# Attention over 64 heads on one core: one PSUM tile for all score buffers, and the order of every engine read from a table

## The chip, the core and the metric

The kernel runs on one core of a Trainium2 chip. A core has five engines, each with its own in-order queue of instructions: TensorE (PE in the profile; PEld are its weight loads), VectorE (DVE), ScalarE (ACT), GpSimd (POOL) and SyncE (SP, which here only issues DMAs). They wait for each other through semaphores. SBUF is the working memory, and PSUM the small memory into which TensorE writes and from which ScalarE and VectorE read. The metric is the device time of one execution in microseconds, lower is better, as the median of several runs.

## The reference

```python
batch, heads, seq, dim = 8, 8, 512, 64          # q, k, v: (8, 8, 512, 64) float32
scale = 1.0 / np.sqrt(dim)
scores = np.einsum('bhqd,bhkd->bhqk', q, k) * scale
scores = scores - scores.max(axis=-1, keepdims=True)
attn = np.exp(scores)
attn = attn / attn.sum(axis=-1, keepdims=True)
out = np.einsum('bhqk,bhkd->bhqd', attn, v)
```

64 independent heads of 512 x 512 attention. The kernel leaves the maximum out, since a constant shift of the scores cancels in the quotient.

## The kernel before

**Tiling.** The 64 heads are taken as 32 pairs g = 0 to 31, with heads a and b. Per head the 512 keys are cut into four chunks c of 128. A block (g, c, head) is a 128 keys x 512 queries piece of the scores; two blocks make a group m, so that a pair has four groups, and group m belongs to pair m // 4. The last group is split into two halves by queries, 127 and 128. A pair in the middle takes its blocks as a0 b0, a1 b1, and so on: the two heads lie on partitions 0 to 63 and 64 to 127, and their two score matmuls run side by side on the two halves of the array. In pairs 0 and 31 the order is a0 a1, a2 a3, b0 b1, b2 b3.

**Steps of a pair.** SyncE loads q, k and v of the pair (256 KB each, seven pairs of buffers each). GpSimd casts them to fp16 (`cast`, L515 and L525). TensorE transposes q and k (`transposes`, L558, two parts of four), and VectorE copies the result from PSUM (`copy`, L571). For each group TensorE makes the scores (`scores`, L598, two matmuls) in a PSUM buffer `st`. There are three such buffers, each 128 x 1024 fp32 (two banks), taken in turn, so the scores of group m wait until group m-3 has been read. Then one engine reads the buffer:

- ScalarE takes the exponential of 110 groups with one ACTIVATE of 128 x 1024 each (L602), into an fp16 tile `pt`.
- For 16 groups, listed in `ON_DVE`, VectorE does it: `raise` (L625) reads PSUM and makes an integer whose bits are a rough 2^x, and five passes (`pass_`, L642 to L665) over fp16 in SBUF make of it two summands, `pe` and `pd`.

**Values.** A unit is 128 queries of one head: four matmuls with `pt` as weights and v, with a column of ones, as the moving side (`values`, L704); a block that VectorE made has two summands, so it takes two matmuls. Seven units share a PSUM bank (tags x0 and x1, two banks in turn; the transposes use them too). VectorE then takes the reciprocal of the sums (`rec`, L671) and multiplies (`mul`, L676) into a ring of results in SBUF, from which SyncE stores. The last head (31 b) has its own four parts (`last_values`, L720), reciprocal (L733), multiplication (L734) and store (L740).

**What sets the order.** Every engine runs the instructions in the order in which the code writes them down. `Plan` writes it: a small simulation in steps of 5 ns with one clock per engine, with prices and rules as constants (`SLOT`, `EXP`, `LATE_COPY`, `HURRY` and others). It decides at each moment which job each engine takes next, and returns the list of steps. The list is played by these lines:

```python
        plan = Plan(groups, NP, 3)
        steps = plan.run()
        ...
        for what, *args in steps:
            do[what](*args)
```

A cast is held behind a VectorE instruction (`cast_behind`, "behind" counts back from the newest), because both engines use the same port of SBUF.

**Waits.** The tile framework adds the semaphores: whoever reads a tile waits for its writer, and whoever takes a buffer again waits for the readers of what was in it. Since each `st` is a tile of its own, two groups in different buffers have no dependence.

Of the kernel before, what the change touches and what calls it, by code (L numbers as in the profile page):

```python
# [17 lines left out]
class Plan:  # L18

    SLOT, EXP, EXP_DONE, EXP_FIXED = 216, 853, 181, 64  # L20
    INTO, OUT_OF = 96, 96
    TRANSPOSE, V_UNIT = 222, 128
    TO_ACT, TO_DVE, TO_PE = 220, 210, 60

    COPY, NORM, RAISE = (601, 690), (50, 133), (1132, 1215)
    RECIPROCAL = 115
    SCALE, PRODUCT, EXTRA = 333, 600, 29
    COPY_1 = (400, 190)
    NORM_COLUMN, PASS_DONE = 67, 115
    PASSES = (SCALE, SCALE, PRODUCT, SCALE, PRODUCT)  # L30
    BITS = 2
    NEEDS = (None, None, 0, 2, 3)
    FIRST_EXP = 5000
    STEP = 5
    CALM, KEEN = 9000, 4
    FIRST_UNIT = 4
    KNOWN, OVER = (13, 15, 18, 20, 22, 24, 27, 42, 50, 61, 69, 97), 6
    ON_DVE = (5, 10, 16, 25, 28, 39, 44, 54, 63, 66, 74, 81, 91, 96, 103, 116)

    LATE_NORM, LATE_COPY, HURRY, SOON, BACKLOG = 700, 1500, 800, 160, 600  # L40
    LATE_MUL, WAIT = 400, 200
    SLACK, AHEAD = 0, 2

    CAST, CAST_PORT, CAST_DONE, TO_POOL = 557, 475, 130, 150
    SCALE_PORT, PRODUCT_PORT, GAP, REACH = 271, 537, 20, 5
    FIRST_LAND, LOAD, STORE, LATENCY, ISSUE = 5200, 752, 376, 2300, 470
    QUEUED, URGENT = 3500, 16
    PAIRED, STORE_ISSUE = 18, 520
    RAW, QK16, NV, NU = 7, 5, 12, 112
    PAIR, DUEK, DUEV, DUEL, PRE = 3300, 3550, 6000, 5000, 0  # L50

    def __init__(self, groups, pairs, first):
        self.groups, self.pairs = groups, pairs
        self.pe, self.act, self.dve = 7000, self.FIRST_EXP, 6300
        self.pool, self.port, self.dma = 4600, 4600, self.FIRST_LAND
        self.m, self.tiled = first, True
        self.read = []
        self.exps = {}
        for m in range(first):
            self.act += self.EXP + self.EXP_FIXED  # L60
            self.exps[m] = self.act + self.EXP_DONE
            self.read.append(self.exps[m])
        self.tq = {0: 5800}
        self.transposed = {0: 5800}
        self.next_t = 1
        self.part_t = 0
        self.banks = [5100, 5800]
        self.todo = [(g, h) for g in range(pairs) for h in range(2)]
        self.last = self.todo.pop()
        self.last_part = 0  # L70
        self.head = None
        self.units = self.FIRST_UNIT
        self.member = {b: m for m, grp in enumerate(groups) for b in grp}
        self.ready = []
        self.passes = []
        self.passed = {}
        self.raised = set()
        self.steps = []
        self.busy_dve = 0
        self.order, self.paired = [], 0  # L80

        late = {grp[0][0] for m, grp in enumerate(groups) if m in self.ON_DVE}
        due = []
        for g in range(pairs):
            scores = 5000 + self.PAIR * g
            if g:
                due += [(scores - self.DUEK, g, "k"), (scores - self.DUEK + 10, g, "q")]
            due.append((scores + self.DUEV + (self.DUEL if g in late else 0), g, "v"))
        self.due = sorted(due)
        self.uncast = list(self.due)  # L90
        self.casts = []
        self.landed, self.cast_done = {}, {}
        self.first_loads = [(g, n) for _, g, n in self.due if g < self.RAW]
        self.first_loads += [(self.RAW, "k"), (self.RAW, "q")]
        for x in self.first_loads:
            self.dma += self.LOAD
            self.landed[x] = self.dma
        self.loads, self.stores, self.stored = [], [], []
        self.sp = 1650 + 470 * len(self.first_loads)

    def note(self, t, *what):
        self.steps.append((t, len(self.steps)) + what)

    def trigger(self, t):

        ops = self.ops
        if not ops or ops[-1][1] <= t - 300:  # L110
            return 1, None
        n = len(ops) - 1
        while (
            n > 0
            and len(ops) - n < self.REACH
            and not ops[n][2]
            and ops[n][0] - ops[n - 1][1] <= self.GAP
        ):
            n -= 1
        if n > 0 and ops[n][0] - ops[n - 1][1] <= self.GAP:  # L120
            n -= 1
        return len(ops) - n, ops[n][1]

    def emit(self, t, back, after):
        _, g, n = self.uncast.pop(0)
        shared = (g, n) == (1, "q")
        self.note(t, "cast", g, n, back if t > self.CALM else 0)
        if not shared:
            self.casts.append((g, n, t if after is None else after + self.TO_POOL))
        if g + self.RAW < self.pairs:  # L130
            self.loads.append((g + self.RAW, n))

    def fits(self, t, soon=0):
        if not self.uncast:
            return False
        _, g, n = self.uncast[0]
        if n != "v" and g >= self.QK16 and self.transposed.get(g - self.QK16, 1e9) > t:
            return False
        return self.landed.get((g, n), 1e9) <= t + soon

    def step_pool(self, t):
        if self.uncast and self.uncast[0][1:] != (1, "q") and not self.casts and self.pool <= t:
            quiet = not self.passes and self.port <= t and not any(x[1] == "raise" for x in self.ready)
            if self.fits(t) and (quiet or self.uncast[0][0] - self.PRE < t):
                self.emit(t, 1, None)
        if self.casts and self.pool <= t and self.port <= t:
            g, n, after = self.casts[0]
            if after <= t and self.landed.get((g, n), 1e9) <= t:
                self.casts.pop(0)
                begin = max(self.pool, self.port, after, self.landed[(g, n)])  # L150
                self.pool = begin + self.CAST
                self.port = begin + self.CAST_PORT
                self.cast_done[(g, n)] = begin + self.CAST + self.CAST_DONE

    def step_sp(self, t):
        if self.sp > t or (self.loads and self.dma > t + self.QUEUED):
            return
        urgent = len(self.stores) > self.URGENT
        if self.loads and not urgent:
            g, n = self.loads[0]  # L160
            if self.cast_done.get((g - self.RAW, n), 1e9) <= t:
                self.loads.pop(0)
                self.note(t, "load", g, n)
                self.dma = max(self.dma, t + self.LATENCY - self.LOAD) + self.LOAD
                self.landed[(g, n)] = self.dma
                self.sp = t + self.ISSUE
                return
        if self.stores and self.stores[0] <= t:
            both = self.both()
            if both and (len(self.stores) < 2 or self.stores[1] > t):  # L170
                return
            heads = 2 if both else 1
            self.note(t, "store", heads)
            self.dma = max(self.dma, t + self.LATENCY - heads * self.STORE) + heads * self.STORE
            for _ in range(heads):
                self.stores.pop(0)
                self.stored.append(self.dma)
            self.paired += heads - 1
            self.sp = t + self.STORE_ISSUE

    def both(self):

        n = len(self.stored)
        g, h, u = self.order[n]
        return (
            self.paired < self.PAIRED
            and g < self.pairs - 2
            and h == 0
            and n + 1 < len(self.order)
            and self.order[n + 1][0] == g  # L190
            and u % self.NU + 8 <= self.NU
        )

    def room(self, t, u):
        heads = (u - self.NU - self.FIRST_UNIT + 3) // 4
        return heads <= 0 or len(self.stored) >= heads and self.stored[heads - 1] <= t

    def free(self, n=0):
        m = self.m + n
        if m >= len(self.groups):  # L200
            return 1e9
        g = self.groups[m][0][0]
        return max(0 if m < 3 else self.read[m - 3], self.tq.get(g, 1e9))

    def for_dve(self, m):
        return m in self.ON_DVE
# [692 lines left out]
```

## Time and profile before

| what | value |
|---|---|
| time, median of 3 runs | 113.66 us (113.52 to 114.11) |
| time of the profiled execution | 113.92 us |
| its span, from first to last instruction | 112.1 us |
| TensorE, VectorE, ScalarE, GpSimd busy | 103.2, 100.8, 105.5, 65.9 us |
| granted TensorE clock, mean | 0.994 |
| moved by DMA | 33.84 MB |

How to read it: a row of the timeline has the start in us, the length in us, the engine, the line and operation, the tiles (written <- read), the shape and how many instructions were merged in the row. In brackets stands how long the engine had been idle before it, and which instruction ended that. An instruction's length covers its whole stay in the engine, so lengths of neighbours overlap. Busy shares near 100% on three engines say that none can be off for long; they do not say which one sets the end.

### The profile page before, as it was taken

Reading aid. Unit: us, or ns where it says so; the run is one execution under the profiler, and the core shown is the slowest. Engines: PE = TensorE matmul, PEld = TensorE weight load, DVE = VectorE, ACT = ScalarE, POOL = GpSimd, SP = SyncE. Lnnn points to the kernel's source line nnn. Section 1 sums busy time; section 2 is a strip of 40 time slices with the busy share of each in tenths; the row PEclk is TensorE's granted clock in tenths of the full one; section 3 lists DMA queues with packets and bytes.
Section 4 is the critical chain, followed back from the end, with each engine's and each line's share of the span. In section 5 each row is a group of like instructions: output and inputs, shape, how many; then the busy total and the mean of one; then the engine's idle time right before and its main releaser. Section 6 shows DMA issues by size and latency. Waiting matters only on the chain.

```text
span 112.1 us, 4408 instructions
## 1 busy us (share of the span) xinstructions
PE 103.2 (92%) x1728; PEld 69.4 (62%) x1728; DVE 100.8 (90%) x227; ACT 105.5 (94%) x118; POOL 65.9 (59%) x127
## 2 busy tenths in 40 slices
PE   7978889999799998999989999899999999999980
PEld 7634555766367766658647767577557577675660
DVE  1647999999999999999999999999999999997390
ACT  4599999999999999999999999999999999999970
POOL 2147768549756886495594786876784855600000
PEclk9999999999999999999999999999999999999997
DMA  3999999999999999999999999999999974142354
GB/s 106 276 359 353 345 350 347 355 336 349 345 347 336 341 346 343 354 364 375 370 358 382 350 355 377 354 372 362 343 366 305 349 245 143 52 141 99 97 167 161
DMA packets 35093, 33.84 MB, mean 302 GB/s; under 512 B 2304, under 2 KB 35072, under 8 KB 35072
## 3 DMA queue, kind: packets, MB, share of 16 engines
q1 hardware_dynamic: 34496, 33.04, 90.4%
q10 hardware_dynamic: 576, 0.52, 1.4%
q8 instruction: 13, 0.21, 0.8%
q14 instruction: 8, 0.07, 0.2%
HBM read 25.17 MB, written 8.39 MB: 299 GB/s over the span
## 4 chain that ended last, share of the span: by engine, by line
DVE 39%; PE 24%; DMA 15%; issue 8%; POOL 7%; SPq 3%; ACT 2%; POOLq 0%; ACTq 0%
PE o L704 13%; DMA v<-in_v_dram 10%; PE st L598 8%; DVE pd L625 8%; DVE tqk L571 7%; DVE ring L676 7%; DMA q<-in_q_dram 5%; DVE m L659 4%; POOL qkp L525 4%; DVE pd L665 4%; POOL vp L515 3%; PE tp L558 2%; SPq L509 2%; DVE m L642 2%; DVE pe L651 2%
## 5 line engine op out<-in xcount | busy, mean ns | idle before, releaser
L602 ACT ACTIVATE pt<-st 128x1024 f16<-128x1024 f32 (+1 forms) x110 | 100.3, 1144 | 0.2 <-PE st L598 0.2
L704 PEld LDWEIGHTS <-pt 128*128 128x128 f16 x880 | 38.8, 98 | 12.1 <-issue 10.2
L704 PE MATMUL o<-vp,pt 128*128 128x65 f16 x880 | 45.3, 194 | 0.4 <-POOL vp L515 0.2
L598 PE MATMUL st<-tqk 64*128 64x512 f16 (+1 forms) x250 | 41.7, 380 | 2.6 <-ACT pt L602 1.4
L525 POOL CAST qkp<-k 128x512 f16<-128x512 f32 x31 | 22.2, 717 | 11.3 <-DVE rc L671 5.3
L525 POOL CAST qkp<-q 128x512 f16<-128x512 f32 x30 | 21.7, 725 | 9.0 <-DVE rc L671 5.3
L515 POOL CAST vp<-v 128x512 f16<-128x512 f32 x32 | 21.4, 679 | 9.2 <-PE st L598 2.4
L676 DVE TENSOR_TENSOR ring<-o,rc 128x448 f32<-128x448 f32 (+2 forms) x37 | 22.3, 606 | 0.4
L704 PE MATMUL o<-vp,pe 128*128 128x65 f16 x128 | 21.8, 194 | 0.0
L704 PE MATMUL o<-vp,pd 128*128 128x65 f16 x128 | 21.7, 192 | 0.0
L558 PE MATMUL tp<-ident,qkp 128*128 128x128 f16 x248 | 19.6, 220 | 1.6 <-DVE tqk L571 0.8
L558 PEld LDWEIGHTS <-qkp 128*128 128x128 f16 x248 | 14.4, 97 | 9.9 <-issue 4.6
L571 DVE COPY tqk<-tp 128x1024 f16<-128x1024 f16 x30 | 20.3, 683 | 0.0
L625 DVE TENSOR_SCALAR pd<-st 128x1024 uint16<-128x1024 f32 x16 | 19.5, 1216 | 0.7 <-PE st L598 0.7
L598 PEld LDWEIGHTS <-tqk 64*128 64x128 f16 x250 | 10.7, 93 | 11.8 <-issue 4.6
L704 PEld LDWEIGHTS <-pe 128*128 128x128 f16 x128 | 12.5, 98 | 3.4 <-issue 3.3
L704 PEld LDWEIGHTS <-pd 128*128 128x128 f16 x128 | 12.5, 98 | 0.0
L659 DVE TENSOR_TENSOR m<-m 128x1024 f16<-128x1024 f16 x16 | 11.0, 685 | 0.0
L665 DVE TENSOR_TENSOR pd<-pd,m 128x1024 f16<-128x1024 f16 x16 | 10.9, 684 | 0.0
L671 DVE RECIPROCAL rc<-o 128x7 f32<-128x7 f32 (+2 forms) x37 | 7.4, 199 | 2.6 <-PE o L704 2.4
L661 DVE TENSOR_SCALAR m<-m 128x1024 f16<-128x1024 f16 x16 | 6.7, 418 | 0.1
L651 DVE TENSOR_SCALAR pe<-pd 128x1024 uint16<-128x1024 uint16 x16 | 6.6, 411 | 0.0
(51 smaller groups left out, 34.9 us busy)
## 6 DMA issues: line engine op xcount, KB each, us to landing
v<-in_v_dram SPq DMA_DIRECT2D x32, 256.0 KB, 5.8
k<-in_k_dram SPq DMA_DIRECT2D x31, 256.0 KB, 5.8
q<-in_q_dram SPq DMA_DIRECT2D x31, 256.0 KB, 5.9
out_dram<-ring SPq DMA_DIRECT2D x18, 256.0 KB, 5.5
out_dram<-ring SPq DMA_DIRECT2D x25, 128.0 KB, 2.2
k<-in_k_dram ACTq DMA_DIRECT2D x2, 128.0 KB, 2.8
q<-in_q_dram SPq DMA_DIRECT2D x2, 128.0 KB, 2.6
out_dram<-ring ACTq DMA_DIRECT2D x2, 128.0 KB, 1.9
```

The lines of the kernel that those rows point to most:

```text
L515: return nc.gpsimd.tensor_copy(out=vps[g % NV][:, :, :, 0:D], in_=raw[g]["v"][:, :, :, :])
L525: return nc.gpsimd.tensor_copy(out=dst, in_=src[:, :, :, :])
L558: reads[g] = nc.tensor.transpose(tps[g][:, n, i, :], qkp[g][:, n, i, :], ident)
L571: nc.vector.tensor_copy(out=tqk[g][:, :, :], in_=tps.pop(g).rearrange("p n i c -> p n (i c)"))
L598: nc.tensor.matmul(st[:, x, cols], kc, qc[:, cols], start=True, stop=True)
L602: ins = nc.scalar.activation(out=pt[:, :, cols], in_=st[:, :, cols], func=EXP, scale=scale, bias=SHIFT)
L625: nc.vector.tensor_scalar(out=r["pd"][:, :, :], in0=r["st"][:, :, :], scalar1=BITS, scalar2=BIAS, op0=AluOp.mult, op1=AluOp.add,)
L651: ins = nc.vector.tensor_scalar(out=r["pe"][:, :, :], in0=u[:, :, :], scalar1=0x7C00, scalar2=None, op0=AluOp.bitwise_and,)
L659: ins = nc.vector.tensor_tensor(out=m16, in0=m16, in1=m16, op=AluOp.mult)
L665: ins = nc.vector.tensor_tensor(out=u16, in0=u16, in1=m16, op=AluOp.mult)
L676: nc.vector.tensor_tensor(out=ring[:, u % NU : u % NU + n, :], in0=o[:, x : x + n, 0:D], in1=rcs.pop(u)[:, 0:n].broadcast_to([P, n, D]), o ...
L704: nc.tensor.matmul(os[u // 7][:, u % 7, :], part[:, y * P : (y + 1) * P], vps[g % NV][:, h, c, :], start=(n == 0), stop=(n == len(parts) - 1),
```

## The change

**The order.** `Plan` goes. A class `Order` holds strings: one letter per step in `STEPS` (S scores, T transposes, V values, C copy, R raise, a to o passes, N reciprocal, M multiplication, K cast, G load, w and W store, L and F the last head), and lists with the pairs that these refer to. `steps()` reads them and yields the same kind of list. All counts are those of before: 126 score steps, 252 units, 62 transposes, 94 casts, 94 loads, 37 reciprocals, 16 raises. The 16 groups on VectorE were 5, 10, 16, 25, 28, 39, 44, 54, 63, 66, 74, 81, 91, 96, 103, 116 and are 5, 11, 16, 25, 28, 39, 45, 54, 62, 66, 75, 82, 91, 96, 108, 118. `SPLIT`, `JOINED` and `WIDE` are empty, so the code that they steer does nothing here. Of the 24 buffers of `pt` 21 are used.

**The last pair** takes its blocks as a0 b0, a1 b1, a2 a3, b2 b3.

**The score buffers.** One PSUM tile `sts` of three times two banks takes the place of three rotating tiles; group m uses part (m + 1) % 3. The framework would tie all users of one tile together, so `at` tells it which pairs of instructions have nothing to do with each other: those that touch different parts, and those of which neither is TensorE's (ScalarE's and VectorE's reads).

```diff
-class Plan:
...
+class Order:
+
+    ON_DVE = (5, 11, 16, 25, 28, 39, 45, 54, 62, 66, 75, 82, 91, 96, 108, 118)
+    SPLIT = ()
+    JOINED = ()
+    SINGLES, DOUBLES = 21, 1
+    PAIR_1 = "a0b0 a1b1 a2b2 a3b3"
+    LAST_PAIR = "a0b0 a1b1 a2a3 b2b3"
...
+    STEPS = (
+        "SKKTTKCSKSSRKTTSCVKVVaSNScVKSMVbTVdTKSCVKRSKTTSCSKeTTVgSKCSGKRVVGSKVGNSfSKMVGVhSTGkVTiVV"
...
+        "VVbVwScVwVVNSdVVeVVSMSVVwVVNVMVVVVSwNSMwVVVVwVVVwSNVMVVVLLwwNLMLFw"
+    )
...
+        for step in self.STEPS:
+            if step == "S":
+                yield "scores", m, m in self.ON_DVE
+                m += 1
...
-    ps_st = ctx.enter_context(tc.tile_pool(name="ps_st", bufs=3, space=bass.MemoryType.PSUM))
+    ps_st = ctx.enter_context(tc.tile_pool(name="ps_st", bufs=1, space=bass.MemoryType.PSUM))
...
+    sts = ps_st.tile([P, 3, 2, S], FP32, tag="st", name="sts")
+    touched = []
+
+    def banks(m):
+        return sts[:, (m + 1) % 3], (m + 1) % 3
+
+    def at(ins, *where, tied=False):
+
+
+        pe = nc.tensor.engine
+        for other, there, also in touched[-200:]:
+            apart = there.isdisjoint(where) and not also
+            both_read = pe not in (other.engine, ins.ins.engine)
+            if other.engine != ins.ins.engine and (apart or both_read):
+                tc.declare_no_dep(ins.ins, other, reason="other banks")
+        touched.append((ins.ins, set(where), tied))
...
-        st = ps_st.tile([P, 2, S], FP32, tag="st", name=f"st_{m}")
+        st, bank = banks(m)
...
-            nc.tensor.matmul(st[:, x, cols], kc, qc[:, cols], start=True, stop=True)
+            at(nc.tensor.matmul(st[:, x, cols], kc, qc[:, cols], start=True, stop=True), bank)
...
-        plan = Plan(groups, NP, 3)
-        steps = plan.run()
+        order = Order()
...
-        for what, *args in steps:
+        for what, *args in order.steps():
             do[what](*args)
```

**What moves, on TensorE near the end.** L598 and L316 are the score matmuls of before and of the changed kernel, L704 and L446 the value matmuls; `tqk_31` holds pair 31, whose first group is 124; `pt`, `pe` and `pd` carry the group's number. "waits" names the engine whose semaphore holds an instruction. Before:

```order
L598 LDWEIGHTS tqk_31_2721
L598 MATMUL st_124_2852<-tqk_31_2721 128x512 [waits Activation_49]
L598 LDWEIGHTS tqk_31_2721
L598 MATMUL st_124_2852<-tqk_31_2721 128x512
L704 LDWEIGHTS pe_116_2700
L704 MATMUL o_33_2822<-vp5_91,pe_116_2700 128x65 [waits Pool_49]
```

The same place of TensorE in the changed kernel:

```order
L316 LDWEIGHTS tqk_31_2609
L316 MATMUL sts_100<-tqk_31_2609 128x512 [waits Activation_49]
L316 LDWEIGHTS tqk_31_2609
L316 MATMUL sts_100<-tqk_31_2609 128x512
L316 LDWEIGHTS tqk_31_2609
L316 MATMUL sts_100<-tqk_31_2609 128x512 [waits Activation_49]
L316 LDWEIGHTS tqk_31_2609
L316 MATMUL sts_100<-tqk_31_2609 128x512
L446 LDWEIGHTS pt_116_2565
L446 MATMUL o_33_2696<-vp5_91,pt_116_2565 128x65 [waits Pool_49]
```

Behind group 124 stood 40 value matmuls and then groups 125, 126 and 127; now group 125 stands ahead of the same 40 matmuls, and 126 and 127 behind them. From there to the end the counts are equal: 32 value matmuls, group 128, 16 value matmuls and 16 of the last head.

**What moves on GpSimd in the first third.** `vp8` is v of pair 8 in fp16, `qkp` holds q and k of the pair whose number stands behind it; L515 and L205 are the casts of v, L525 and L215 those of q and k. Before:

```order
L525 CAST qkp_10_785<-q32_10_623 128x2x4x64
L515 CAST vp6_92<-v32_6_144 128x8x64
L515 CAST vp8_94<-v32_8_731 128x8x64
L543 MEMSET mark_99 1x1
L525 CAST qkp_11_927<-k32_11_649 128x2x4x64
L525 CAST qkp_11_927<-q32_11_672 128x2x4x64
```

In the changed kernel:

```order
L215 CAST qkp_11_810<-q32_11_604 128x2x4x64
L233 MEMSET mark_99 1x1
L215 CAST qkp_12_948<-k32_12_736 128x2x4x64
L205 CAST vp8_94<-v32_8_791 128x8x64
L215 CAST qkp_12_948<-q32_12_643 128x2x4x64
L205 CAST vp7_93<-v32_7_583 128x8x64
```

The cast of v of pair 8 is row 42 of GpSimd before and row 49 now; its load is row 34 of SyncE before and row 41 now.

More of the change, by code (lines that the diff above doesn't have):

```diff
@@ L623, in raise_ @@
         r = raised[m]
[L624 to L633 removed]
+        for n in ("pe", "pd"):
+            r[n] = dpool.tile([P, 2, S], U16, tag=n, name=f"{n}_{m}")
+        own = r["own"]
+        for x, b in enumerate(groups[m]):
+            if x >= own:
+                blocks[b] = [r[n].bitcast(FP16)[:, x, :] for n in ("pe", "pd")]
+        ins = nc.vector.tensor_scalar(
+            out=r["pd"][:, own:2, :],
+            in0=r["st"][:, own:2, :],
+            scalar1=BITS,
+            scalar2=BIAS,
+            op0=AluOp.mult,
+            op1=AluOp.add,
+        )
+        at(ins, r["bank"])
+        dve(ins)
     def pass_(m, s):
@@ L727, in last_values @@
                 )
+                for halves in () if late else last["exps"]:
+                    tc.declare_no_dep(ins.ins, halves, reason="other banks")
     def finish():
```

602 lines of the change are left out of this document (158 added, 444 removed), and 13 rows, old and new, of tables (CASTS, HEADS, LOADS).

## The prediction

> **What bounds the kernel now.** I read the page's busy shares first, then the busy time by stretches of the span, then the timelines of ScalarE, TensorE and VectorE at the start and at the end.
>
> ```profile
> PE 103.2 (92%) x1728; PEld 69.4 (62%) x1728; DVE 100.8 (90%) x227; ACT 105.5 (94%) x118; POOL 65.9 (59%) x127
> ...
> L602 ACT ACTIVATE pt<-st 128x1024 f16<-128x1024 f32 (+1 forms) x110 | 100.3, 1144 | 0.2 <-PE st L598 0.2
> ```
>
> Three engines are above 90%, so the shares do not decide. Idle time does: ScalarE was idle 0.2 us in all ahead of its 110 exponentials. The stretch from 9.4 to 104 us says the same, and its ScalarE timeline shows the pace (start, length, count):
>
> ```profile
> 9.40:104.00 94.60, 91.14 (x1542) 60.81 (x1541) 93.30 (x192) 94.60 (x104) 62.61 (x117) 1.00 0.98 321
> ...
> 101.86 1.99 ACT L602 ACTIVATE pt<-st 128x1024 f16<-128x1024 f32 x2
> ...
> 102.76 2.00 ACT L602 ACTIVATE pt<-st 128x1024 f16<-128x1024 f32 x2
> ...
> 103.66 1.10 ACT L602 ACTIVATE pt<-st 128x1024 f16<-128x1024 f32 x1
> ```
>
> ScalarE is busy 94.60 of 94.60 us. The rows' ends (start plus length) are 103.85 and 104.76: exponentials end 0.91 to 0.92 us apart, and 0.92 is also (100.3 - 2 x 0.49)/108 over the whole kernel, taking the two halves at 0.49. So ScalarE runs without a hole, and a length above 0.92 only means that it took its next instruction early. Its work is not changed (110 ACTIVATEs of the same shapes, 16 groups elsewhere). What the change can win lies ahead of this train or behind it. Ahead of it:
>
> ```profile
> 7.37 0.29 DVE L523 CAST qkp<-q 128x256 f16<-128x256 f32 x1 [1.15 <-DMA q<-in_q_dram]
> ...
> 7.98 1.06 ACT L602 ACTIVATE pt<-st 128x1024 f16<-128x1024 f32 x1
> ...
> 8.78 0.82 PE L598 MATMUL st<-tqk 64*128 64x512 f16 x6 [0.52 <-DVE tqk L565]
> ...
> 9.21 5.65 ACT L602 ACTIVATE pt<-st 128x1024 f16<-128x1024 f32 x6 [0.18 <-PE st L598]
> ```
>
> One pause: exponentials start at 7.98 and 9.21, 1.23 apart where 0.92 would do, so 0.31 us are lost. They wait for the first scores of pair 1, these for VectorE's copy, and that for the load of q of pair 1. Behind the train:
>
> ```profile
> 102.58 0.98 PE L598 MATMUL st<-tqk 64*128 64x512 f16 x4
> 102.98 0.09 PEld L598 LDWEIGHTS <-tqk 64*128 64x128 f16 x1 [0.29 <-issue]
> 103.50 0.10 PEld L704 LDWEIGHTS <-pe 128*128 128x128 f16 x1 [0.42 <-issue]
> ...
> 104.87 0.61 PE L598 MATMUL st<-tqk 64*128 64x512 f16 x4
> 105.73 0.38 PE L598 MATMUL st<-tqk 64*128 64x256 f16 x2 [0.25 <-ACT pt L602]
> 106.04 1.20 PE L704 MATMUL o<-vp,pt 128*128 128x65 f16 x32
> 106.37 0.20 DVE L671 RECIPROCAL rc<-o 128x7 f32<-128x7 f32 x1 [1.48 <-PE o L704]
> ...
> 107.17 0.39 PE L598 MATMUL st<-tqk 64*128 64x256 f16 x2
> ...
> 107.49 0.68 PE L704 MATMUL o<-vp,pt 128*128 128x65 f16 x16
> ...
> 108.01 0.84 PE L720 MATMUL o_last<-vp,pt 128*128 128x65 f16 x16
> ...
> 108.21 0.18 DVE L671 RECIPROCAL rc<-o 128x4 f32<-128x4 f32 x1
> 108.43 0.42 DVE L676 TENSOR_TENSOR ring<-o,rc 128x256 f32<-128x256 f32 x1
> 108.89 0.18 DVE L733 RECIPROCAL rc_last<-o_last 128x4 f32<-128x4 f32 x1
> 109.10 0.42 DVE L734 TENSOR_TENSOR obl<-o_last,rc_last 128x256 f32<-128x256 f32 x1
> 109.55 0.33 SPq L740 DMA_DIRECT2D out_dram<-obl  x1
> ```
>
> The tail after the last exponential is one chain: group 128's scores at 107.17, 16 value matmuls, 16 of the last head, VectorE's reciprocal and multiplication twice, the last store. At 108.89 VectorE starts the last reciprocal as the multiplication ahead of it (108.43 + 0.42) and the last matmuls (108.01 + 0.84) both end at 108.85.
>
> **The change, part by part.**
>
> *The score tile.* The order with its waits shows that the scores of a group wait for the reader of group m-3 in both kernels, each ACTIVATE for its own scores (and, as before, for its own long past output buffer or a cast), and each raise for its own scores. Before, different buffers were different tiles, so no wait between ScalarE's and VectorE's reads existed; the declarations only undo what merging the tiles would add. 0 us, both bounds 0. With 21 instead of 24 output buffers every exponential's TensorE wait is still on its own scores, so 0 us.
>
> *The start.* The first 21 loads are issued in the same order, and the first transposes and copies follow them as before. I keep the pause: 0 us; the bounds are -0.31 (it goes) and 0.
>
> *The tail.* All from the rows above. A lone score group costs: 32 value matmuls from 106.04 take (1.20 - 0.19)/31 = 0.033 each, 0.19 being the length of one, so they are issued by 107.08; group 128 starts at 107.17, and the next value matmul at 107.49. So 0.09 to go in and 0.32 to come out. Group 124, two matmuls of the same head before, took 103.50 - 102.98 = 0.52, 0.2 more, since two of one head cannot share the array. Before: 124 at 102.98, the 40 value matmuls from 103.50, 125 at 104.87, and 127 at 105.73, which waited for its buffer. After: 125 stands ahead of the 40, and its buffer is that of group 122, whose exponential ends at 101.86 + 1.99 = 103.85. With 0.05 of semaphore 125 starts at 103.90. Then 103.90 + 0.32 = 104.22 for the values, + 40 x 0.033 + 0.09 = 105.63 for group 126 (two of one head, 0.43), 106.06 for 127, 106.37 for its values where 106.04 stood. That is 0.3 us late, nothing between there and the last store waits for anything that could take it up (TensorE's queue, then VectorE's in the order of before), and the last exponential, which needs group 128 at 107.50 instead of 107.17, starts 0.4 later than that, 107.9, just when ScalarE is free. So +0.30 us. Bounds: 0, if the chain after the last exponential were slack, which the touching 108.85s exclude but for some 0.05, and 0.52, if group 125 came with both the waits and TensorE's own delay.
>
> *TensorE's switches.* The order has 87 runs of score groups between other work where it had 74. A group alone costs 0.41 beyond its neighbours (0.09 + 0.32) and one more in a run 0.22 (the four matmuls in 0.61, less a length of 0.39), so 13 more runs cost 13 x 0.19 = 2.5 us on TensorE. What hides it is TensorE's slack:
>
> ```profile
> L704 PE MATMUL o<-vp,pt 128*128 128x65 f16 x880 | 45.3, 194 | 0.4 <-POOL vp L515 0.2
> ...
> L704 PE MATMUL o<-vp,pe 128*128 128x65 f16 x128 | 21.8, 194 | 0.0
> L704 PE MATMUL o<-vp,pd 128*128 128x65 f16 x128 | 21.7, 192 | 0.0
> L558 PE MATMUL tp<-ident,qkp 128*128 128x128 f16 x248 | 19.6, 220 | 1.6 <-DVE tqk L571 0.8
> ...
> 9.54 0.62 PE L558 MATMUL tp<-ident,qkp 128*128 128x128 f16 x8
> ```
>
> 1136 value matmuls x 0.033 = 37.5, 248 transposes x (0.62 - 0.22)/7 = 0.057 make 14.1, 126 groups x 0.22 = 27.7, 74 runs x 0.19 = 14.1: 93.4 us of issue between 6.5 and 108.85, that is 9 us free of 102. After: 6.5 free. On the whole it fits, so the sum holds 0; locally a score may come late. Bounds 0 and 2.5; I take 0.10, near the lower end, as there the order itself can be added up (first rival).
>
> The Trainium skill, TensorEngine Tiling (Array Packing), Key Properties, says that changing the tiling mode drains TensorE. The 0.41 against 0.22 agrees with it. By that rule alone, with nothing to hide it, the sum would be 2.5 us higher.
>
> *VectorE.* The same instructions. Its idle time near the end (1.48 in the row at 106.37) is the cover of its 93.3 busy in 94.6: an order that loses under 1 us there costs nothing. The last raise comes two groups later, its passes still end ahead of group 124. 0 us.
>
> *Casts and loads.* Of what is moved past SP's and POOL's queues v of pair 8 is nearest to a wait:
>
> ```profile
> 30.67 1.57 POOL L515 CAST vp<-v 128x512 f16<-128x512 f32 x2 [0.46 <-DVE pe L651]
> ...
> 36.70 0.60 POOL L525 CAST qkp<-k 128x512 f16<-128x512 f32 x1
> 37.25 0.61 POOL L525 CAST qkp<-q 128x512 f16<-128x512 f32 x1
> ...
> 32.25 0.37 SPq L509 DMA_DIRECT2D q<-in_q_dram  x1
> 33.00 0.37 SPq L509 DMA_DIRECT2D v<-in_v_dram  x1
> ```
>
> The load stands 7 places later, at 0.75 each 5.3 us; before, the data were there for the second cast of the row at 30.67 (30.67 + 1.57 - 0.61 = 31.6), so they are there by 36.9. The cast now stands where 36.70 or 37.25 stood. It may wait 0 to 0.2 us, and TensorE, which wants it within one exponential, as long. I take 0.
>
> **The sum**, on the profiled execution: 113.92 + 0.30 + 0.10 = 114.32 us. That execution is 0.26 above the median, so on the median 113.66 + 0.40 = 114.06, called 114.1, or +0.35%. Some 0.5% (0.57 us) is what a measurement of this kernel tells from no change: same is 113.09 to 114.23.
>
> **The rivals.**
>
> 1. *TensorE's order starves ScalarE in the middle: slower.* A score reaches its exponential 0.43 after its start (8.78 to 9.21), an exponential lasts 1.06, so scores later than 0.43 + 1.06 - 0.92 = 0.57 ahead of the previous one's end open a hole. Ordinarily the buffer comes free 2 x 0.92 earlier, but with a VectorE group among the last two only 0.92 earlier: a window of 0.92 - 0.57 - 0.05 = 0.30 us. Behind group 108 now stand 20 value matmuls, 109, 19 value matmuls, 110. From 108 at its earliest that is 0.41 + 0.66 = 1.07 and 0.41 + 0.63 = 1.04, against 2 x 0.92 = 1.84: 110 comes 0.27 into its 0.30. For: several places of the new order are that tight when added up in this way, of the old one none has under 0.1. Against: all fit. Five or more misses of 0.1 to 0.2 give +0.7 instead of 0.10, 114.7; it decides from 0.27 us of holes (114.23). Chance 0.33.
> 2. *A cast comes late and TensorE stands before it: slower.* Pair 8's v above; late in the program k of pair 29 is cast right ahead of its transposes. At 0.2 to 0.6 us per miss, 114.4. Chance 0.10.
> 3. *The tail is taken up, and the pause at the start goes: faster at best.* 113.66 - 0.31 = 113.35. The load order speaks against it. For a gain over 0.5% even the whole pause is too small. Chance 0.10.
>
> That the change does not do what it says holds for the waits: there were none. It is in the forecast.
>
> **How the numbers follow.** Forecast 0.47, rivals 0.33, 0.10, 0.10. Slower: nearly all of rival 1, most of rival 2, and a tenth of the forecast's, 0.43. Faster by over 0.5%: 0.04, a part of rival 3. Same: 0.53. The range goes from 113.4 (rival 3) to 115.2 (rival 1 with some 1.2 us of holes). The forecast's own is 113.8 to 114.3.
>
> **What would show it.** Right: ScalarE still without a hole from 9 to 104 us, busy time of exponentials 100.3; the first pause at 7.98 as before; on TensorE group 125 at its buffer's release and group 128 some 0.3 nearer to the end of the last exponential; the last two reciprocals 0.3 further from it. Wrong: idle time before ACTIVATEs, or ends more than 0.92 apart, in the middle, above all around the groups 56, 53, 110 and 120; GpSimd waiting for v of pair 8 or TensorE for GpSimd; a shorter pause at the start.

## Result and the profile after

The changed kernel takes 114.83 us (median, 114.62 to 115.87) where the kernel before took 113.64 in the same comparison: 1.0121 times as long, interval 1.0078 to 1.0163. The forecast of 114.1 said slower by too little, and 114.83 lies above the 114.23 up to which the prediction counted a time as the same, but inside its range. Each ratio here and below, with its 95% interval, leaves out executions over 1.5% above the fastest of their kernel, and so is not simply the quotient of the two medians beside it. The profiled execution of the changed kernel took 114.62 us, the least of its runs, and its span is 112.8 us against 112.1. The sections behind this one take the time apart.

From the page of the changed kernel, the busy line, the shares of the chain that ended last, and two groups (busy us, mean ns of one, idle before):

```profile
PE 104.8 (93%) x1728; PEld 70.5 (62%) x1728; DVE 102.6 (91%) x227; ACT 105.9 (94%) x118; POOL 63.3 (56%) x127
...
DVE 63%; ACT 16%; PE 10%; issue 5%; POOL 3%; POOLq 0%; ACTq 0%
...
L332 ACT ACTIVATE pt<-sts 128x1024 f16<-128x1024 f32 (+1 forms) x110 | 100.7, 1055 | 0.5 <-PE sts L316 0.3 <-ACT pt L332 0.2
...
L401 DVE TENSOR_TENSOR m<-m 128x1024 f16<-128x1024 f16 x16 | 11.8, 739 | 0.0
```

The chain and the same pass (c, the squaring) of the kernel before:

```profile
DVE 39%; PE 24%; DMA 15%; issue 8%; POOL 7%; SPq 3%; ACT 2%; POOLq 0%; ACTq 0%
...
L659 DVE TENSOR_TENSOR m<-m 128x1024 f16<-128x1024 f16 x16 | 11.0, 685 | 0.0
```

The chain now goes through VectorE for 63% of the span where it did for 39%, and one of VectorE's passes is 54 ns longer on the mean, although nothing in it has changed. ScalarE has idle time, which it did not have: its row of the stretch from 9.4 to 104 us (busy us by engine, in the order PE, PEld, DVE, ACT, POOL) and its timeline around 34 and 39 us:

```profile
9.40:104.00 94.60, 91.69 (x1518) 61.07 (x1517) 93.67 (x191) 94.10 (x103) 59.62 (x116) 1.00 0.99 320
...
32.73 1.13 ACT L332 ACTIVATE pt<-sts 128x1024 f16<-128x1024 f32 x1
34.19 4.69 ACT L332 ACTIVATE pt<-sts 128x1024 f16<-128x1024 f32 x5 [0.33 <-PE sts L316]
39.05 2.85 ACT L332 ACTIVATE pt<-sts 128x1024 f16<-128x1024 f32 x3 [0.17 <-ACT pt L332]
```

A busy engine's idle time understates what a hole costs, because exponentials in the train overlap by some 0.14 us and behind a hole they do not. I therefore take each hole from the ends of two exponentials that follow each other in the trace, less the 0.917 us of the train. In the profile of the changed kernel this gives, behind the start:

| hole ahead of group | at (us) | us |
|---|---|---|
| 12 and 13 | 14.5 | 0.11 |
| 36 | 34.2 | 0.44 |
| 42 | 39.0 | 0.28 |
| 77, 98, 105, 110, 114, 120 | 66.6 to 101.6 | 0.02 to 0.06 each, 0.26 together |

Together 1.08 us; the profile of before has none behind 12 us. The hole ahead of group 12 varies between executions: 0.09 to 0.28 us in the profiles of programs that are the same up to there. The others repeat. The end, in the changed kernel (ScalarE's last row, the scores of groups 126 and 127, the values behind them, the scores of group 128, the last head's matmuls, the last reciprocal):

```profile
106.17 2.97 ACT L332 ACTIVATE pt<-sts 128x1024 f16<-128x1024 f32 x4
106.24 0.60 PE L316 MATMUL sts<-tqk 64*128 64x512 f16 x4
106.78 0.62 PE L446 MATMUL o<-vp,pt 128*128 128x65 f16 x14
...
107.90 0.39 PE L316 MATMUL sts<-tqk 64*128 64x256 f16 x2
...
108.74 0.86 PE L461 MATMUL sts<-vp,pt 128*128 128x65 f16 x16
...
109.64 0.18 DVE L476 RECIPROCAL rc_last<-sts 128x4 f32<-128x4 f32 x1
```

and before:

```profile
105.57 2.92 ACT L602 ACTIVATE pt<-st 128x1024 f16<-128x1024 f32 x4
```

The last exponential ends at 109.14 and the last reciprocal starts 0.50 later; before it was 108.49 and 0.40 (108.89, shown with the prediction). So the tail is 0.10 us longer. 1.08 + 0.10 = 1.18 us, beside a difference of the medians of 1.19. That they agree so closely is luck, since the interval of the ratio leaves 0.9 to 1.9 us. The spans differ by only 0.7, because the pause at the start, 0.34 us in the profile of before, is missing in this execution of the changed kernel. That pause was between 0 and 0.8 us in the profiles of both orders that follow, and I leave it out of the comparisons.

What stands ahead of the largest hole? VectorE, GpSimd and TensorE of the changed kernel between 29 and 34 us:

```profile
29.51 0.61 DVE L418 TENSOR_TENSOR ring<-o,rc 128x448 f32<-128x448 f32 x1
30.04 1.11 DVE L401 TENSOR_TENSOR m<-m 128x1024 f16<-128x1024 f16 x1
31.08 1.27 DVE L261 COPY tqk<-tp 128x1024 f16<-128x1024 f16 x2
...
29.24 0.81 POOL L215 CAST qkp<-q 128x512 f16<-128x512 f32 x1 [0.60 <-DVE pd L407]
30.01 0.61 POOL L205 CAST vp<-v 128x512 f16<-128x512 f32 x1
30.60 1.03 POOL L215 CAST qkp<-k 128x512 f16<-128x512 f32 x1
...
31.81 0.42 PE L446 MATMUL o<-vp,pt 128*128 128x65 f16 x8 [0.69 <-DVE tqk L261]
...
33.70 0.61 PE L316 MATMUL sts<-tqk 64*128 64x512 f16 x4
```

The cast of v of pair 6 starts at 30.01, pass c of group 25 starts at 30.04 and takes 1.11 us instead of 0.68. The copies behind it come 0.43 later, TensorE stands 0.69 us for the bank that they read, its scores for group 36 start at 33.70, and the exponential starts at 34.19. In the kernel before the same cast started at 30.67 (shown with the prediction), 0.15 us *inside* that pass; there the cast took 1.01 us and the pass its usual time:

```profile
30.52 0.69 DVE L659 TENSOR_TENSOR m<-m 128x1024 f16<-128x1024 f16 x1
```

The Trainium skill, GPSIMD Engine Reference, 1. Specifications, says that GpSimd's SBUF interfaces are shared with VectorE and contended by instructions in a two-port mode or with two SBUF inputs. The rows agree: pass c has two inputs in SBUF, and casts beside VectorE's reads of PSUM take their 0.61. That the one which comes first is not the one that waits is read here from the rows.

### The profile page after: what moved, and what is told of

Read it like the earlier page. It is cut to its first block, busy times and chain, and to the rows that moved or that the text cites. A ratio compares the mean times of both kernels' runs of the same rounds, so it can differ in the third digit from the quotient of the medians.

```text
span 112.8 us, 4369 instructions
## 1 busy us (share of the span) xinstructions
PE 104.8 (93%) x1728; PEld 70.5 (62%) x1728; DVE 102.6 (91%) x227; ACT 105.9 (94%) x118; POOL 63.3 (56%) x127
## 4 chain that ended last, share of the span: by engine, by line
DVE 63%; ACT 16%; PE 10%; issue 5%; POOL 3%; POOLq 0%; ACTq 0%
ACT pt L332 13%; DVE pd L363 13%; DVE tqk L261 13%; DVE ring L418 11%; DVE pd L407 7%; DVE m L401 6%; DVE m L403 3%; DVE pe L393 3%; DVE m L384 3%; DVE rc L413 3%; PE o L446 3%; PE sts L316 3%; PE sts L495 3%; ACT pt L545 3%; PE tp L248 2%
## 5 line engine op out<-in xcount | busy, mean ns | idle before, releaser
L332 ACT ACTIVATE pt<-sts 128x1024 f16<-128x1024 f32 (+1 forms) x110 | 100.7, 1055 | 0.5 <-PE sts L316 0.3
L446 PEld LDWEIGHTS <-pt 128*128 128x128 f16 x880 | 39.8, 98 | 15.9 <-issue 13.4
L446 PE MATMUL o<-vp,pt 128*128 128x65 f16 x880 | 48.6, 195 | 1.1 <-DVE tqk L261 0.7
L316 PE MATMUL sts<-tqk 64*128 64x512 f16 (+1 forms) x250 | 42.9, 381 | 1.7 <-ACT pt L332 0.8
L215 POOL CAST qkp<-k 128x512 f16<-128x512 f32 x31 | 21.3, 686 | 12.9 <-DVE pe L393 2.6
L205 POOL CAST vp<-v 128x512 f16<-128x512 f32 x32 | 21.2, 670 | 10.3 <-DVE pd L407 2.5
L215 POOL CAST qkp<-q 128x512 f16<-128x512 f32 x30 | 19.9, 668 | 11.5 <-DVE rc L413 4.4
L446 PE MATMUL o<-vp,pe 128*128 128x65 f16 x128 | 22.1, 194 | 0.0
L446 PE MATMUL o<-vp,pd 128*128 128x65 f16 x128 | 22.0, 192 | 0.0
L248 PE MATMUL tp<-ident,qkp 128*128 128x128 f16 x248 | 20.8, 220 | 0.8 <-POOL qkp L215 0.3
L363 DVE TENSOR_SCALAR pd<-sts 128x1024 uint16<-128x1024 f32 x16 | 19.4, 1215 | 0.7 <-PE sts L316 0.7
L316 PEld LDWEIGHTS <-tqk 64*128 64x128 f16 x250 | 11.5, 93 | 10.4 <-issue 2.4
L446 PEld LDWEIGHTS <-pe 128*128 128x128 f16 x128 | 12.5, 98 | 2.2 <-issue 2.1
L446 PEld LDWEIGHTS <-pd 128*128 128x128 f16 x128 | 12.5, 98 | 0.0
L401 DVE TENSOR_TENSOR m<-m 128x1024 f16<-128x1024 f16 x16 | 11.8, 739 | 0.0
(45 smaller groups left out, 34.2 us busy)
```

Of the source, the lines that this page charges most:

```text
L205: return nc.gpsimd.tensor_copy(out=vps[g % NV][:, :, :, 0:D], in_=raw[g]["v"][:, :, :, :])
L215: return nc.gpsimd.tensor_copy(out=dst, in_=src[:, :, :, :])
L248: reads[g] = nc.tensor.transpose(tps[g][:, n, i, :], qkp[g][:, n, i, :], ident)
L316: at(nc.tensor.matmul(st[:, x, cols], kc, qc[:, cols], start=True, stop=True), bank)
L332: ins = nc.scalar.activation(out=pt[:, 0:own, cols], in_=st[:, 0:own, cols], func=EXP, scale=scale, bias=SHIFT)
L363: ins = nc.vector.tensor_scalar(out=r["pd"][:, own:2, :], in0=r["st"][:, own:2, :], scalar1=BITS, scalar2=BIAS, op0=AluOp.mult, op1=AluOp.add,
```

## Experiments

Theory A: casts that are under way when a pass of VectorE starts make the pass longer; VectorE is full, so the delay goes through banks and buffers to ScalarE. Theory B: TensorE's new order itself starves ScalarE. Theory C: the merged score tile and its waits. Theory D came up for group 42: see there.

### The new order on the old tiles, and the old order on the new tile

```diff
...
-        plan = Plan(groups, NP, 3)
-        steps = plan.run()
+        steps = Order().steps()
...
```

> The kernel before, with its own three rotating score tiles, playing the new table of steps (with 21 output buffers and the new last pair). Theory A (GpSimd's casts now run into VectorE's passes, VectorE falls behind and TensorE and ScalarE wait for it) and theory B (TensorE's new order itself starves ScalarE) both put the loss into the order: about 114.8 us, within 0.3 of the changed kernel. Theory C (the merged score tile and its waits) expects the time of before, 113.65.

Measured 114.57 us against 113.80, ratio 1.0059 (1.0038 to 1.0079). Its profile has the holes ahead of groups 12 (0.18) and 36 (0.44) and most of the small ones; that of group 42 is missing.

```diff
...
-        for what, *args in order.steps():
+        plan = Plan(groups, NP, 3)
+        steps = plan.run()
+        for what, *args in steps:
```

> The changed kernel with its one score tile and its declarations, playing the steps that the planner of before writes (24 output buffers, the old last pair). A and B expect the time of before, 113.65 within 0.2; C expects the time of the changed kernel, 114.8.

Measured 114.05, ratio 1.0031 (1.0005 to 1.0057): a little more than A and B expected, far less than C. Behind the start its ScalarE has no hole at all:

```profile
11.74 96.84 ACT L742 ACTIVATE pt<-sts 128x1024 f16<-128x1024 f32 x106
```

105 full exponentials at 0.917 and a half one at 0.49 make 96.8. But the last reciprocal again starts 0.50 us behind the last exponential (0.40 with the old tiles in the run above). So the order makes the holes, and the tile makes the 0.10 us of the tail.

### One cast

```diff
-        ... 10q3 6v4 11k3 ...
+        ... 10q3 6v2 11k3 ...
```

> The changed kernel with one number different: the cast of v of pair 6 waits for the multiplication ahead of the squaring pass of group 25 instead of for a reciprocal two instructions earlier, so that it begins inside that pass and not just ahead of it. Theory A: the pass at about 30.0 us takes 0.68 us again instead of 1.11, TensorE's idle 0.69 us at 31.8 shrinks to about 0.25, ScalarE's hole of 0.44 us at 34.2 goes, and the time falls by 0.3 to 0.7, to 114.1 to 114.5. Theory B: the hole stays at 0.3 or more and the time at 114.8.

Measured 114.66, ratio 1.0083 (1.0052 to 1.0113). VectorE, GpSimd and TensorE at the same place, and ScalarE:

```profile
30.50 0.68 DVE L401 TENSOR_TENSOR m<-m 128x1024 f16<-128x1024 f16 x1
...
30.64 1.01 POOL L205 CAST vp<-v 128x512 f16<-128x512 f32 x1
...
31.83 0.42 PE L446 MATMUL o<-vp,pt 128*128 128x65 f16 x8 [0.25 <-DVE tqk L261]
...
28.64 10.26 ACT L332 ACTIVATE pt<-sts 128x1024 f16<-128x1024 f32 x11
39.22 1.94 ACT L332 ACTIVATE pt<-sts 128x1024 f16<-128x1024 f32 x2 [0.33 <-PE sts L316]
```

The pass takes 0.68, TensorE stands 0.25 where it stood 0.69, and the hole ahead of group 36 is gone: theory A, in every row that it named. Its time was missed, 114.66 where 114.5 was the most: the next hole, ahead of group 42, takes up part of the gain, 0.43 where it was 0.28, because TensorE was as late there as before and ScalarE now arrives earlier.

### More work on VectorE in the kernel before

```diff
         dve(ins)
+        if s == 1 and m in (28, 44, 63, 81):
+            latest[0] = nc.vector.tensor_scalar(
+                out=r["pe"][:, :, :], in0=u[:, :, :],
+                scalar1=0x7C00, scalar2=None, op0=AluOp.bitwise_and)
```

> The kernel before with the pass that cuts out the exponent done twice (same result) in groups 28, 44, 63 and 81: 4 x 0.33 = 1.3 us more of VectorE, nothing else. Theory A (no slack of VectorE in the middle; what it loses there reaches ScalarE): ScalarE gets holes behind those places, and the time rises by 0.4 to 1.3 us, to 114.05 to 114.95. The working of the prediction (VectorE's idle 0.88 and 1.48 us near the end cover what it loses): 113.65, within 0.15.

Measured 116.38 us, ratio 1.0211 (1.0174 to 1.0247). VectorE at the first of the four places and near the end:

```profile
33.68 0.38 DVE L651 TENSOR_SCALAR pe<-pd 128x1024 uint16<-128x1024 uint16 x1
34.09 0.72 DVE L668 TENSOR_SCALAR pe<-pd 128x1024 uint16<-128x1024 uint16 x1
34.73 0.61 DVE L684 TENSOR_TENSOR ring<-o,rc 128x448 f32<-128x448 f32 x1
...
106.14 0.21 DVE L679 RECIPROCAL rc<-o 128x7 f32<-128x7 f32 x1 [0.89 <-PE o L712]
...
108.48 0.21 DVE L679 RECIPROCAL rc<-o 128x7 f32<-128x7 f32 x1 [1.48 <-PE o L712]
```

The added passes cost more than I had reckoned. Each started only 0.03 us behind the end of the pass that it repeats, while neighbours in VectorE's rows usually overlap by some 0.09, and two of the four met a cast and took 0.72 us instead of 0.43. From the first pass to the next other instruction 1.05, 0.80, 0.80 and 1.09 us where one pass takes 0.29 to 0.34, so 2.4 us in all. ScalarE's holes behind the start add up to 2.28. What VectorE loses in the middle is lost nearly one for one. And the idle time near the end, which the prediction had taken as cover, is still there, 0.89 and 1.48: it is a wait for the tail, not slack.

### One instruction ahead of the 64th

The changed kernel again, as a measure for its edits:

> The changed kernel once more, beside the edits of it that follow, and for a second profile of it. If the holes in ScalarE's train belong to the order of the program they stand where they stood: about 0.44 us ahead of group 36 (34.2 us), 0.28 ahead of group 42 (39.0 us), some 0.25 in seven small ones behind 66 us. If they are chance, elsewhere. The pause at the start may differ (0 or 0.3 us). Time 1.2% over the kernel before.

Measured 114.98 against 113.89, ratio 1.0093 (1.0068 to 1.0118). Its second profile has the same holes at the same groups, within 0.03 us each: 0.13 ahead of 12 and 13, 0.44, 0.29, and 0.27 in the six small ones. They belong to the program; only the size of the first differs more in the profiles further on.

The hole ahead of group 42 needed an explanation of its own. Its scores start at 38.22 and its exponential at 39.05, 0.83 later, where 0.43 to 0.49 is usual for an exponential that waits for its scores (33.70 to 34.19 above). All that it waits for was done by 38.61, when the first two of these matmuls had ended (0.39 us for a pair):

```profile
38.22 0.61 PE L316 MATMUL sts<-tqk 64*128 64x512 f16 x4
```

ScalarE's instructions at this place, as the trace has them, counted from 1:

```
62 ACTIVATE group 41
63 semaphore wait (scores of group 42, an exponential long past)
64 ACTIVATE group 42 (waits for a cast that ended at 31.6 us)
```

In the run of the new order on the old tiles one instruction more stands ahead of it, and there the exponential started 0.04 us behind the semaphore wait instead of 0.36. Hence theory D, and this edit:

```diff
         nc.scalar.copy(k16[:, 1], tk[:, 1])
+        spare = cpool.tile([P, 1], FP16, name="spare")
+        nc.scalar.copy(spare[:, 0:1], tk[:, 1, 0, 0:1])
```

> The changed kernel with one more ScalarE instruction of one column ahead of the first exponential. In two profiles the exponential of group 42 starts 0.36 us after the end of the semaphore instruction ahead of it, where others take 0.045; it is ScalarE's 64th instruction there, and in the kernel before with the new table, where it is the 65th, it takes 0.04. Theory D (each 64th instruction arrives late if nothing hides it): as the 65th it starts 0.04 after, the hole at 39.0 us shrinks from 0.28 to under 0.05, time 0.2 to 0.3 us less than the changed kernel. If it is the third wait of that exponential (theory C), the hole stays.

Measured 115.05, ratio 1.0109 (1.0076 to 1.0142). ScalarE's rows:

```profile
32.15 2.03 ACT L332 ACTIVATE pt<-sts 128x1024 f16<-128x1024 f32 x2
34.52 7.44 ACT L332 ACTIVATE pt<-sts 128x1024 f16<-128x1024 f32 x8 [0.34 <-PE sts L316]
```

Eight exponentials follow each other from 34.52 without a break; the hole is gone, with the same three waits on that exponential. So at this place the lag depends on where the instruction stands in ScalarE's queue, not on its waits. The time did not fall measurably: 0.28 us is 0.25%, and the intervals are wider than that. In this profile the holes ahead of groups 12 and 13 were 0.25 instead of 0.13, and one of 0.05 came up ahead of group 49. Why number 64 comes late no run shows, nor whether each further 64th does.

### Both edits, and group 125

> Both edits in the changed kernel: the cast of v of pair 6 begins inside the squaring pass of group 25, and one more ScalarE instruction at the start. Theories A and D: no hole at group 36 and at most 0.15 at group 42 (TensorE is 0.1 late there), time 0.4 to 0.7 us less than the changed kernel. Theory B (TensorE's order is the cause): both holes stay, no change.

Measured 114.34 against 113.89, ratio 1.0045 (1.0024 to 1.0065), where the changed kernel beside it had 1.0093. Both holes are gone:

```profile
28.54 16.73 ACT L332 ACTIVATE pt<-sts 128x1024 f16<-128x1024 f32 x18
```

About half of the loss is thus undone by one number and one instruction.

```diff
-        ... VSMSVVwVVNVMVVVVSwNSMw ...
+        ... VSMVVwVVNVMVVVVSSwNSMw ...
```

> The changed kernel with the scores of group 125 put behind the 40 value matmuls again, as before the change. The step of the prediction that puts 0.30 us there: 0.3 us less than the changed kernel. If ScalarE's last exponential sets the end and group 128 still comes in time for it (it came 0.12 us early): 0.0 to 0.1 less, or none.

Measured 115.47, ratio 1.0139 (1.0110 to 1.0168): slower than the changed kernel, which neither expectation had. ScalarE and the scores near the end:

```profile
102.57 4.69 ACT L332 ACTIVATE pt<-sts 128x1024 f16<-128x1024 f32 x5
107.58 2.92 ACT L332 ACTIVATE pt<-sts 128x1024 f16<-128x1024 f32 x4 [0.32 <-PE sts L316]
...
105.23 0.39 PE L316 MATMUL sts<-tqk 64*128 64x512 f16 x2
107.15 0.82 PE L316 MATMUL sts<-tqk 64*128 64x512 f16 x6
```

Behind the values group 125 is too late (107.15), and a hole of 0.43 us opens. In the kernel before the same place did no harm, because there group 124 started as soon as its buffer was free (102.98 against 102.93). In this table TensorE is already behind: group 124 starts at 105.23 where its buffer is free at 104.51. So the place that group 125 was given is needed.

### The early cast, the tail, and what TensorE does

```diff
-        ... 3k2 3q5 4k2 ...
+        ... 3k2 3q2 4k2 ...
...
-                for halves in () if late else last["exps"]:
+                for halves in last["exps"][1:] if late > half else () if late else last["exps"]:
```

These two come on top of both edits above.

> The kernel of the two edits (cast of v of pair 6 later, one more ScalarE instruction) with two more: the cast of q of pair 3 waits for the reciprocal ahead of the first squaring pass instead of for the first raise, and the third part of the last head is declared free of the last half exponential, whose bank and columns it does not touch. Theory A: that pass takes 0.68 us where it took 0.98, and ScalarE's hole of 0.09 to 0.28 us ahead of group 12 falls below 0.1. The merged tile's own price: the last reciprocal starts 0.40 us behind the end of the last exponential where it started 0.50. Together 0.15 to 0.3 us less than without these two; about 114.1 where the kernel before takes 113.85.

Measured 114.34 against 113.70, ratio 1.0051 (1.0028 to 1.0075). In the rows both expectations hold: pass c of group 5, and the end (last exponential, last reciprocal):

```profile
11.16 0.69 DVE L401 TENSOR_TENSOR m<-m 128x1024 f16<-128x1024 f16 x1
...
106.48 2.06 ACT L332 ACTIVATE pt<-sts 128x1024 f16<-128x1024 f32 x3
...
108.93 0.18 DVE L476 RECIPROCAL rc_last<-sts 128x4 f32<-128x4 f32 x1
```

0.69 where it was 0.98, no hole ahead of group 12, and the last reciprocal 0.39 behind the last exponential (108.54). The time is not measurably below that of the run with two edits; a hole of 0.13 has come up ahead of group 42 in exchange. GpSimd and TensorE show its cause:

```profile
36.76 0.62 POOL L205 CAST vp<-v 128x512 f16<-128x512 f32 x1 [0.19 <-DMA v<-in_v_dram]
...
37.43 0.54 PE L446 MATMUL o<-vp,pt 128*128 128x65 f16 x12 [0.31 <-POOL vp L205]
```

This is v of pair 8, whose load the change moved seven places back: now that the engines are no longer late for other reasons, the cast waits for it.

```diff
-                blocks[b] = [r[n].bitcast(FP16)[:, x, :] for n in ("pe", "pd")]
+                names = ("pd",) if m >= 62 else ("pe", "pd")
+                blocks[b] = [r[n].bitcast(FP16)[:, x, :] for n in names]
```

> The kernel of the two edits with less work on TensorE: from group 62 on the value matmuls leave out the summand pe of VectorE's groups (10 groups, 80 matmuls, 2.6 us), all else the same. Theory B for what is left: ScalarE's six holes of 0.03 to 0.06 us behind 66 us, 0.26 us together, go, at least most of them, and the time falls by 0.2 to 0.3. If late casts or VectorE make them, they stay.

Measured 114.22 against 113.70, ratio 1.0035 (1.0018 to 1.0052). The time did not fall measurably. It was 8 groups and 64 matmuls (1664 where 1728 were), 2.1 us, not the 10 and 80 that I had counted. ScalarE's last 56 exponentials, of the kernel with both edits and of this one:

```profile
57.90 50.94 ACT L332 ACTIVATE pt<-sts 128x1024 f16<-128x1024 f32 x56
```

```profile
58.95 50.80 ACT L332 ACTIVATE pt<-sts 128x1024 f16<-128x1024 f32 x56
```

Five of the six small holes are gone (0.22 us), and the sixth, ahead of group 105, has grown from 0.03 to 0.13. So five are theory B, TensorE's tight order; the sixth does not come from the amount of TensorE's work. Whether it is the casts of pairs 28 and 29, which stand there in the chain of waits, was not tried.

### The collision put into the kernel before

```diff
         steps = plan.run()
+        n = [s[:3] for s in steps].index(("cast", 6, "v"))
+        steps[n] = ("cast", 6, "v", 3)
```

> The kernel before with one number different: the cast of v of pair 6 waits for the multiplication ahead of the exponent pass of group 25 instead of for that pass, so that it is under way when the squaring pass starts. Theory A: that pass takes 0.9 to 1.0 us instead of 0.685, VectorE is 0.2 to 0.3 us late from there on, ScalarE gets a hole of 0.05 to 0.3 us within the next ten groups, and the time rises by as much. The working of the prediction, where VectorE's idle time near the end covers it: no hole and no change.

Measured 114.32 against 113.70, ratio 1.0036 (1.0011 to 1.0061). VectorE at that place:

```profile
30.26 0.42 DVE L651 TENSOR_SCALAR pe<-pd 128x1024 uint16<-128x1024 uint16 x1
30.59 1.10 DVE L659 TENSOR_TENSOR m<-m 128x1024 f16<-128x1024 f16 x1
```

The pass takes 1.10 where it took 0.69, and ScalarE has holes of 0.20, 0.11, 0.05, 0.03 and 0.13 ahead of groups 36 to 46 (34.1 to 41.8 us). 0.20 us of holes ahead of the edited place, at 24.7 to 29.4 us, are not the edit's. The profile shows what stands ahead of them:

```profile
21.41 0.61 POOL L525 CAST qkp<-k 128x512 f16<-128x512 f32 x1 [0.80 <-DMA k<-in_k_dram]
...
21.56 1.00 DVE L665 TENSOR_TENSOR pd<-pd,m 128x1024 f16<-128x1024 f16 x1
```

In this execution a cast of k waited 0.80 us for its load, and so was under way when a pass of VectorE started: 1.00 us, where the same pass took 0.68 in the profile of before. It is the same collision once more, brought about by a late load and not by the order. So part of what one execution loses is chance.

### All of them beside each other

Holes behind the start in each profile, with 0.10 us where the merged tile holds the last head, in per cent of 113.7, and the measured ratio:

| kernel | holes + tail, us | % | measured ratio |
|---|---|---|---|
| new tile, old order | 0 + 0.10 | 0.1 | 1.0031 (1.0005 to 1.0057) |
| four edits | 0.41 + 0 | 0.4 | 1.0051 (1.0028 to 1.0075) |
| less on TensorE | 0.48 + 0.10 | 0.5 | 1.0035 (1.0018 to 1.0052) |
| two edits | 0.50 + 0.10 | 0.5 | 1.0045 (1.0024 to 1.0065) |
| before, one cast | 0.71 + 0 | 0.6 | 1.0036 (1.0011 to 1.0061) |
| new order, old tiles | 0.91 + 0 | 0.8 | 1.0059 (1.0038 to 1.0079) |
| changed, one cast | 0.98 + 0.10 | 1.0 | 1.0083 (1.0052 to 1.0113) |
| changed, one more instruction | 1.01 + 0.10 | 1.0 | 1.0109 (1.0076 to 1.0142) |
| changed, first and second comparison | 1.08, 1.13 + 0.10 | 1.0, 1.1 | 1.0121 (1.0078 to 1.0163), 1.0093 (1.0068 to 1.0118) |
| changed, group 125 behind | 1.74 + 0.10 | 1.6 | 1.0139 (1.0110 to 1.0168) |
| before, passes twice | 2.28 + 0 | 2.0 | 1.0211 (1.0174 to 1.0247) |

The measured loss follows ScalarE's holes within 0.3%, over a range of 2%. Each row has the holes of a single execution beside the time of several. No version beats the kernel before.

## Why the prediction was only half right

The bound was read rightly: ScalarE's train sets the time, and what the change could do was to open holes in it. Five terms of the sum were off, and one was missing.

- *VectorE, 0 us.* This step failed, and it is the costliest. I took the idle 1.48 us near the end as cover for what VectorE loses earlier, up to 1 us. The doubled passes (2.4 us lost, 2.28 us of holes) and the collision put into the kernel before show that VectorE has no slack in the middle.
- *Casts and loads, 0 us.* I asked only whether a cast comes late. What the change moved was also where casts start against VectorE's passes, and that is the loss which VectorE could not cover: 0.44 us ahead of group 36 and 0.11 ahead of groups 12 and 13, each undone by the hold of one cast. Ahead of group 12 it is the cast of q of pair 3; it met pass c in most profiles (0.98 us) and pass a in that with one more instruction (0.88 us instead of 0.44). The longest passes were in neither sum nor rivals, although the kernel holds its casts behind VectorE for just this reason.
- *The tail, +0.30.* The order costs nothing there: group 128 started 0.56 us ahead of its exponential (107.90, and 108.46 in the trace), which needs some 0.43, so it was in time; with the new order on the old tiles the last reciprocal stood 0.40 us behind the last exponential, as before; and putting group 125 back makes the kernel slower. I had counted 0.43 + 0.32 = 0.75 us from the start of group 126 to the values behind group 127, where the trace has 0.54 (106.24 to 106.78), and had let the lateness of TensorE run on to the end, although the last exponential sets it.
- *The score tile, 0 us with both bounds 0.* Wrong by 0.10: in the merged tile the third part of the last head waits for the last half exponential, which it does not need. I had looked at the waits of scores, exponentials and raises, not at those of the last head.
- *TensorE's switches, +0.10.* The mechanism was right and the size too small: 0.26 us in six holes, of which the relief of TensorE took away five (0.22). Of the groups named 110 and 120 have holes, and 53 and 56 stayed whole.
- *The 64th instruction, 0.28 us,* was not thought of.

The late cast of v of pair 8 (rival 2) came out at 0.19 us of waiting, within its 0 to 0.2, but only after the holes ahead of it had been taken away; it left a hole of 0.13. That 114.83 lies in the range, near the 114.7 of rival 1 (TensorE's order starves ScalarE), is in part luck: of the 1.18 us only the 0.26 of the small holes are that rival's, and the +0.30 of the tail, three quarters of the forecast's 0.40, was not there. The start was put at 0; the pause comes and goes between executions, so no run decides that.

## What to carry to other kernels

Where one engine runs without a hole, ask of every other engine in the middle whether its delay has anywhere to go; idle time at the end of the program is no cover for work ahead of it. When a change moves work between GpSimd and VectorE, lay the new starts of GpSimd's instructions against VectorE's, and let a cast begin just inside a pass rather than just ahead of it. Holes hide each other: after one is taken away, the next delay, which was there all along, takes part of the gain.

## What I had not expected of the hardware

- A cast under way delays VectorE's pass: one that started 0.03 us behind the cast took 1.11 us instead of 0.68. A cast that starts 0.15 us inside the pass takes 1.01 instead of 0.61, and the pass keeps its 0.68. What counts is how much of the cast is left when the pass starts. Over all profiles pass c took 0.67 to 0.70 us with up to 0.16 left, 0.76 to 0.78 with 0.21 to 0.24, 0.87 with 0.33, 0.97 or 0.98 with 0.43 or 0.44, and 1.10 to 1.12 with 0.56 to 0.58: it is longer by what is left, less some 0.14.
- ScalarE's instruction number 64 (counted from 1 in the trace) started 0.36 us behind the semaphore wait ahead of it, where 0.045 is usual, in the four profiles of programs with this count, and 0.04 in the five in which one instruction more made it number 65.
- Most holes of one program repeat to 0.03 us from one execution to another, while the pause at the start varies by 0.5 or more, and with it the hole ahead of group 12.
